# A decoder block on one core: input loads of the gates' stage ahead of weight stores, and the projection's result stores on ScalarE's queue

## The chip, the core and the metric

The kernel runs on one core of a Trainium2 chip. A core has a matrix engine (TensorE, PE in the profile, with its weight loads as PEld), a vector engine (VectorE, DVE), a scalar engine (ScalarE, ACT), GpSimd (POOL) and SyncE (SP), which here does nothing but issue DMAs. Each engine works through its own instructions in order and waits on semaphores for the others. An instruction that issues a DMA stands in its engine's order like any other; the transfer itself is done by 16 DMA engines that all queues share. The metric is the device time of one launch in microseconds. Before the change the median of three runs is 2417.23 us (2416.68 to 2417.39).

## The reference, cut to what matters

One layer of a decoder, sequence 2048, width 1024, float32:

```python
h = rmsnorm(x, attn_norm)
z = h @ w_in              # pool channels | q | k | v | gate_pool | gate_attn
a = pool_mixer(u_pool, w_pool, pool_scale)       # windows 2, 4, 8, 16
b = swa_sink_attention(q, k, v, sinks)           # window 128, 16 heads, 2 kv heads
x = x + (g_pool * a + g_attn * b) @ w_out        # g_* = sigmoid(gates + b_gate)
h = rmsnorm(x, ffn_norm)
up = causal_depthwise_conv(h @ w_up, conv_w, conv_b)   # 2 x 2816 channels, width 3
x = x + (silu(gate) * val) @ w_down
```

The two places that the change touches are the product that gives the gates (`z[..., o4:]`, two halves of 1024 columns) and the product with `w_out` with the residual added.

## The kernel before

The sequence is worked in two chunks (c = 0, 1) of T = 1024 tokens, channels on the 128 partitions and tokens along the free axis. Every float32 product is done as three products of reduced-precision halves: ACT copies the high half of an operand (a CAST row), DVE subtracts it from the whole to get the low half, and PE multiplies, for each block of the contraction in turn, high by high, high by low and low (of the weights) by high. A weight or an input that reaches PE thus passes a load, ACT and DVE first. Stages per chunk: keys and values, attention items with pieces of other projections between them, the gates, the output projection, the convolved up projection, the down projection.

**Order and buffers.** A scheduler places the instructions of each engine by priorities and costs, from the order in which the program is written; what it decided is fixed at build time. Tiles come from pools, and a new tile takes a buffer of its pool as soon as the tile there before it has had its last reader; its load waits for that reader. The pools that matter: "U" (19 buffers of 1 MB: input tiles, split weights and split inputs), "M" (5), and "R" (3, raw weights on their way in). All loads and stores but GpSimd's accumulating ones go through `load` (L239), that is, in the order of SP's queue: a store that waits for its result holds every load written behind it.

**The gates' stage** (`gates`, L1418; `Gates` and `Up` are the unit of work). A unit is one block of 128 gate channels, `units` has the blocks 5, 2, 3, 0, 1 in chunk 0. A unit's two products (pool gate and attention gate, over 1024 tokens) are done as one Strassen-like scheme of seven products, named `one` to `seven`, of weights A11, A12, A22, S1 to S4 and of inputs B11, B21, B22, T1 to T4. The input halves T1 to T4 are sums of the four input tiles of the chunk (`xg`, two 128-channel blocks each), which are loaded again from `xT`, scaled by the norm's gain on ACT (`scale_input`, L1415), added on DVE (`right_t1`, L1144; `right_t2`, L1153; `right_t3`, L1160; `right_t4`, L1170) and split into halves (`parted`, L1043 on ACT and L1044 on DVE). Tiles 0 and 1 are loaded during the last attention items (`mixer`, n = 4 and 5), tiles 2 and 3 in `gates`. PE's first products there that need tiles 2 and 3 are `three` (with T2), `five` (T3) and `seven` (T4).

In chunk 0 the weight blocks of the first two units are made in the last attention items (`units[f].w.step`, in `mixer`) and written to DRAM (`store`), to be fetched again in chunk 1 without being split again. The weights' pieces: A11 with A12 (one U tile, stored as `kept_A`), A22 (an M tile, also `kept_A`), S3 with S2 and S1 with S4 (U tiles, `kept_S`). `store` writes every piece that is made and not yet written.

**The output projection** (`out_proj`, L1055). For n = 0, 1 (halves of 512 tokens) and m = 0 to 7 (blocks of 128 channels): get the split weights of block m, 24 matmuls into a PSUM bank, add half of it to the residual on DVE (L1096), scale on ACT (L1098), square on ACT (L650, for the next norm), store the 256 KB result to `x2d` (L1105, a row of L239 on SP). The raw weights of w_out arrive in R tiles some blocks ahead and are split by L245 (ACT, twice 512 columns) and L246 (DVE). In chunk 0 it also makes the blocks of two up-projection weights (loads `U<-w_up`, steps at L358 and L359, stores `kept_A`, `kept_S`). In the trace's names, the raw weights of m = 4, 5 and 6 of n = 0 are the R tiles 5006, 5053 and 5103, and the results of m = 2, 3 and 4 are the M tiles 5041, 5090 and 5136.

Of the kernel before, what the change touches and what calls it, by code (L numbers as in the profile page):

```python
# [218 lines left out]
def block_kernel(ctx: ExitStack, tc: tile.TileContext, x, xT, pos, vec, qkn, w_poolT, w_pool, w_q, w_kv,  # L219
                 w_gp, w_ga, w_out, w_up, w_down, outT):  # L220
    nc = tc.nc
    V, G, A = nc.vector, nc.gpsimd, nc.scalar
# [15 lines left out]
    def load(dst, src):  # L238
        nc.sync.dma_start(dst, src)  # L239
# [813 lines left out]
    x2d = dp.tile([8, P, T], F32, "x2d")  # L1053

    def out_proj(c, ms, mixes):  # L1055

        xg = [up_.tile([P, 2, T], F32, "U") for _ in range(4)]
        norms = []

        def residual(j):  # L1060
            load(xg[j], xT[2 * j * P:(2 * j + 2) * P, c * T:(c + 1) * T]
                 .rearrange("(k p) t -> p k t", p=P))

        residual(0)
        heads = [Kept(f) for f in PRE]
        for n in range(2):
            acc = fp.tile([P, 512], F32, "F")
            c_ = slice(n * 512, (n + 1) * 512)
            for m in range(KT):
                if n == 0 and m % 2 == 0 and m < 6:  # L1070
                    residual(m // 2 + 1)
                w = stream.get("out", m)
                for f, at in PRE.items() if c == n == 0 else ():
                    if m == at:
                        raw = up_.tile([P, 2, 8, P], F32, "U")
                        load(raw[:, 0], w_up[f])
                        load(raw[:, 1], w_up[FT + f])
                        made = Blocks([raw[:, 0], raw[:, 1]])
                    elif at < m < at + 3:
                        made.step(2)  # L1080
                    elif m == at + 3:
                        made.store(f)
                if n == 0 and m == 3:
                    mixes[0] = mixed(0)
                if n == 0 and m > 3:
                    ms[7 - m].append(parted(mixes.pop(7 - m)[:, :, N1]))
                if n == 1 and m >= 6:
                    heads[m - 6].fetch("A11", "A12")
                if n == 1 and m == 7:
                    stream.ahead().step(1)  # L1090
                po = ps.tile([P, 512], F32, "f")
                mm3(po, [(w[:, 0, k, :], w[:, 1, k, :], ms[k // 2][n][:, 0, k % 2, :],
                          ms[k // 2][n][:, 1, k % 2, :])
                         for k in (6, 7, 4, 5, 2, 3, 0, 1)])
                x2 = mp.tile([P, 512], F32, "M")
                V.scalar_tensor_tensor(x2, po, 0.5, xg[m // 2][:, m % 2, c_], op0=ALU.mult,  # L1096
                                       op1=ALU.add)
                A.activation(xg[m // 2][:, m % 2, c_], x2, AF.Identity,  # L1098
                             scale=vc[:, V_FN + m:V_FN + m + 1])
                if m < 7 or n == 0:  # L1100
                    square_in(acc, x2, m == 0)
                else:
                    sq = mp.tile([P, 512], F32, "M")
                    A.square(sq, x2)
                load(x2d[m][:, c_], x2)  # L1105
                stream.part(stream.used + 2)
                if n == 1 and m == 1:
                    norms[0]()
                if n == 1 and m == 3:
                    pb, b = norms[1](), {}  # L1110
                if n == 1 and m >= 3 and m < 7:
                    right_first(xg, b, m - 3, pb)

            accs = [acc, sq] if n else [acc]

            def stats(n=n, accs=accs):
                rstd(accs, r2[:, 4 * n:4 * n + 4])

            def whole(n=n):
                return spread(r2[:, 4 * n:4 * n + 4], None)  # L1120

            norms += [stats, whole]
        return xg, b, norms[2:], heads
# [281 lines left out]
    def load_input(c, j):  # L1405

        t = up_.tile([P, 2, T], F32, "U")
        load(t, xT[2 * j * P:(2 * j + 2) * P, c * T:(c + 1) * T]
             .rearrange("(k p) t -> p k t", p=P))
        return t  # L1410
# [7 lines left out]
    def gates(c, units, b, xg, last_probabilities, last_values, last_filler):  # L1418


        def weights(f, n):
            if f < len(units):
                if units[f].w is None:
                    units[f].w = stream.get("gates", units[f].f)
                w = units[f].w
                w.step(n)
                if c == 0 and f < 2:
                    w.store(units[f].f)
                if n and w.at == 4:
                    stream.fetch(stream.used + (1 if f + 1 < len(units) else 2))  # L1430

        def parts(f, *names):
            if c > 0:
                units[f].w.fetch(*names)

        u0, u1, u2 = units[:3]
        if c > 0:
            u2.one("t")
        else:
            weights(1, 1)  # L1440
            last_filler()
        last_probabilities()
        last_values(-2)
        run_later(9)
        right_t1(xg, b, None, (1,))
        if c > 0:
            u2.two()
        last_values(-1)
        run_later(9)
        xg += [load_input(c, j) for j in (2, 3)]  # L1450
        parts(0, "S3", "S2")
        parts(1, "S3", "S2")
        if c > 0:
            weights(2, 1)
        u0.four()
        u0.early()
        for j in (2, 3):
            scale_input(xg[j], j)
        parts(0, "A22")
        t2s = right_t2(xg, b, None)  # L1460
        u1.four("a")
        u1.early()
        right_t3(xg, b)
        u0.three()
        u0.six()
        weights(2 if c > 0 else 1, 1)
        u0.five()
        right_t4(xg, b, t2s)
        parts(1, "A22")
        u0.fetch()  # L1470
        u1.three()
        u1.six()
        u0.attn()
        u0.seven()
        u0.value()
        if c == 0:
            weights(2, 1)
        u1.five()
        u0.combine()
        weights(2, 1)  # L1480
        n = len(units)
        for f in range(2, n):
            u, old = units[f], units[f - 1]
            if f > 2 or c == 0:
                u.one()
                u.two()
            if f == 2 and c == 0:
                weights(2, 2)
            old.fetch()
            old.attn()  # L1490
            weights(f + 1, 1)
            if f == n - 1:
                mixes = {j: mixed(j) for j in (3, 2, 1)}
            old.seven()
            old.value()
            weights(f + 1, 1)
            u.three()
            u.four()
            old.combine()
            if f == n - 1:  # L1500
                ms = {j: [parted(mixes[j][:, :, N0])] for j in (3, 2, 1)}
                x0 = up_.tile([P, 2, 2, 512], F32R, "U")
                old.parts(x0)
                stream.part(stream.used + 2)
            weights(f + 1, 1)
            u.five()
            u.early()
            u.six()
            weights(f + 1, 1)
        u.fetch()  # L1510
        u.attn()
        u.value(N1)
        u.seven()
        u.value(N0)
        for c_ in (N0, N1):
            u.combine(c_)
            if c_ == N0:
                u.parts(x0)
        ms[0] = [x0]
        return ms, mixes  # L1520
# [144 lines left out]
    def mixer(c, hs, kvw):  # L1665
# [48 lines left out]
        xg = []  # L1714
        for i in range(len(items)):
# [15 lines left out]
            if group == 3:  # L1731
                if c == 0:
                    if n == 0:
                        stream.fetch(stream.used + 2)
                    for f, steps in enumerate(({1: 1, 2: 2, 3: 1}, {5: 1, 7: 1})):
                        if n in steps:
                            with tc.issue_after(chain):
                                units[f].w.step(steps[n])
                            units[f].w.store(units[f].f)
                    if n == 4:  # L1740
                        stream.fetch(stream.used + 1)
                elif n < 5:
                    if n == 2:
                        stream.fetch(stream.used + 2)
                    if n > 2:
                        units[n - 3].w = Kept(units[n - 3].f)
                        units[n - 3].w.fetch("A11", "A12")
                elif n == 5:
                    units[2].w = stream.get("gates", units[2].f)
                    units[2].w.step(1)  # L1750
                else:
                    units[n - 6].w.fetch("S1", "S4")
# [118 lines left out]
```

## Time and profile before

| | us |
|---|---|
| median of 3 runs | 2417.23 |
| the profiled execution | 2413.23 |
| its span, first to last instruction | 2411.5 |
| PE busy | 2374.3 (98%) |
| DVE busy | 1886.6 (78%) |
| ACT busy | 1180.3 (49%) |
| POOL busy | 176.4 (7%) |
| mean DMA share over 380 to 440 / 505 to 600 | 0.64 / 0.80 |

Engine times are busy times within the span of one profiled execution. A row of the timeline gives the start and length in microseconds, the engine (SPq is the queue of SyncE), the line, the operation, the tiles out and in with their shapes, the count of like instructions that were put together, and in brackets the idle time before the row with what ended it. A row of the windows gives the window, its length, then busy time and count of PE, PEld, DVE, ACT and POOL, the granted clock of PE (1.00 is full speed), the DMA engines' share and GB/s. Times are from the span's start.

### The profile page before, as it was taken

What the parts mean: (1) busy time and instruction counts of PE and PEld (TensorE: products, weight loads), DVE (VectorE), ACT (ScalarE), POOL (GpSimd) and SP (SyncE); (2) the same over time, 40 slices, a digit from 0 to 9 for tenths busy, and PEclk for the clock granted to TensorE, in tenths of its full rate; (3) what the DMA queues carried; (4) which work ended last, traced back from release to release, by engine and by line L of the source; (5) the groups of instructions that cost most, each with busy time, mean ns of one, the idle gap of its engine ahead of it and who ended that gap; (6) DMA issues with size and microseconds to landing.
All of it is one profiled execution on the core that took longest, in us unless ns stands there. A gap on an engine that the chain in (4) does not pass through costs nothing.

```text
span 2411.5 us, 30292 instructions
## 1 busy us (share of the span) xinstructions
PE 2374.3 (98%) x11120; PEld 1969.9 (82%) x11120; DVE 1886.6 (78%) x2916; ACT 1180.3 (49%) x2169; POOL 176.4 (7%) x122
## 2 busy tenths in 40 slices
PE   8999998999999999999999999999999999999999
PEld 7888887777888888888888888888888888888887
DVE  8687886967877777799955877788588777779994
ACT  7455454555555555543522543455445445554431
POOL 1123121000000000000002142200000000000000
PEclk9999999999999999999999999999999999999999
DMA  9767777596322233546234576667642222228421
GB/s 342 244 199 239 228 216 259 173 348 246 104 99 79 88 107 116 178 163 205 88 140 156 165 223 183 197 208 242 208 158 93 93 80 79 79 71 288 140 70 53
DMA packets 160165, 400.77 MB, mean 166 GB/s; under 512 B 13840, under 2 KB 50192, under 8 KB 150288
## 3 DMA queue, kind: packets, MB, share of 16 engines
q1 hardware_dynamic: 155232, 390.25, 47.7%
q0 software_dynamic: 4352, 8.39, 2.2%
q8 instruction: 87, 1.43, 0.2%
q14 instruction: 62, 0.51, 0.1%
q10 hardware_dynamic: 432, 0.19, 0.0%
HBM read 264.17 MB, written 134.61 MB: 165 GB/s over the span
## 4 chain that ended last, share of the span: by engine, by line
PE 55%; DVE 1%; DMA 1%; ACT 0%; issue 0%; POOL 0%; SPq 0%; DVEq 0%; ACTq 0%; POOLq 0%
PE f L262 12%; PE f L1177 12%; PE t L1177 7%; PE f L1646 4%; PE a L1646 4%; PE s L1646 4%; PE t L1646 4%; PE a L1177 4%; PE a L934 1%; PE a L262 1%; PE s L873 1%; PE t L906 1%; DMA U<-made_pg 0%; DVE F L990 0%; ACT Q L892 0%; DMA U<-w_down 0%
## 5 line engine op out<-in xcount | busy, mean ns | idle before, releaser
L262 PE MATMUL f<-U,U 128*128 128x512 f32 (+1 forms) x2856 | 668.6, 390 | 11.1 <-ACT U L245 6.3
L262 PEld LDWEIGHTS f<-U,U 128*128 128x128 f32 x2856 | 524.6, 188 | 121.0 <-ACT U L245 7.5
L1177 PE MATMUL f<-U,U 128*128 128x512 f32 x1872 | 449.9, 391 | 9.6 <-ACT U L1043 7.5
L1177 PEld LDWEIGHTS f<-U,U 128*128 128x128 f32 x1872 | 352.6, 189 | 85.8 <-ACT U L1043 7.9
L1243 DVE SCALAR_TENSOR_TENSOR M<-F,vc,M 128x1024 f32<-128x1024 f32 x176 | 225.1, 1281 | 140.5 <-ACT M L1240 140.2
L1177 PE MATMUL t<-U,U 128*128 128x512 f32 x1332 | 315.0, 390 | 0.5 <-ACT Q L1195 0.4
L1177 PEld LDWEIGHTS t<-U,U 128*128 128x128 f32 x1332 | 249.5, 188 | 53.9 <-ACT Q L1195 1.2
L358 ACT CAST U<-R 128x1024 fp32r<-128x1024 f32 x147 | 153.5, 1053 | 81.9 <-DVE R L379 40.0
L1177 PE MATMUL a<-U,U 128*128 128x512 f32 x756 | 184.3, 390 | 1.4 <-ACT Q L1195 1.4
L359 DVE TENSOR_TENSOR U<-R,U 128x1024 fp32r<-128x1024 f32 x147 | 179.0, 1221 | 1.4 <-ACT U L358 1.4
L1177 PEld LDWEIGHTS a<-U,U 128*128 128x128 f32 x756 | 141.2, 188 | 31.6 <-ACT Q L1195 2.3
L1177 PE MATMUL f<-U,M 128*128 128x512 f32 x624 | 151.0, 389 | 0.3 <-DVE F L1221 0.3
L892 ACT ACTIVATE Q<-s,st,rq 128x128 f32<-128x128 f32 x256 | 114.0, 456 | 65.6 <-DVE st L889 61.1
L1177 PEld LDWEIGHTS f<-U,M 128*128 128x128 f32 x624 | 117.0, 188 | 25.0 <-DVE F L1221 0.8
L914 POOL TENSOR_SCALAR_AFFINE_SELECT M<-M 128x1024 fp32r<-128x1024 f32 x64 | 94.4, 1475 | 379.4 <-DVE st L894 213.3
L1229 ACT COPY F<-f 128x512 f32<-128x512 f32 x52 | 30.6, 588 | 184.1 <-PE f L1177 183.9
L1604 ACT CAST U<-U 128x1024 fp32r<-128x1024 f32 x76 | 79.0, 1051 | 83.4 <-PE s L1646 21.6
L1240 ACT ACTIVATE M<-F,vc 128x1024 f32<-128x1024 f32 x88 | 109.4, 1243 | 2.0 <-DVE F L1225 0.5
L1605 DVE TENSOR_TENSOR U<-U,U 128x1024 fp32r<-128x1024 f32 x76 | 91.9, 1218 | 3.5 <-ACT U L1604 3.2
L1604 ACT CAST F<-U 128x1024 fp32r<-128x1024 f32 x44 | 46.2, 1051 | 93.7 <-PE a L1646 64.0
L941 ACT COPY U<-a 128x512 f32<-128x512 f32 x64 | 37.5, 586 | 107.1 <-PE a L934 106.9
L246 DVE TENSOR_TENSOR U<-R,U 128x512 fp32r<-128x512 f32 x122 | 82.9, 705 | 9.0 <-ACT U L245 8.7
(283 smaller groups left out, 3715.2 us busy)
## 6 DMA issues: line engine op xcount, KB each, us to landing
R<-w_up SPq DMA_DIRECT2D x80, 512.0 KB, 3.7
actd<-M SPq DMA_DIRECT2D x44, 512.0 KB, 2.6
U<-w_down SPq DMA_DIRECT2D x88, 256.0 KB, 4.9
U<-actd SPq DMA_DIRECT2D x88, 256.0 KB, 5.2
qd<-U SPq DMA_DIRECT2D x64, 256.0 KB, 3.8
Q<-qd SPq DMA_DIRECT2D x64, 256.0 KB, 4.8
U<-xT SPq DMA_DIRECT2D x16, 1024.0 KB, 8.6
R<-w_out SPq DMA_DIRECT2D x32, 512.0 KB, 4.8
```

Source lines behind the costliest of these rows:

```text
L246: low = V.tensor_sub(lo[:, t], src[:, t], hi[:, t].bitcast(F32))
L262: nc.tensor.matmul(out, a, b, start=(i == 0), stop=(i == n - 1))
L358: A.copy(t[:, 0], raw)
L359: V.tensor_sub(t[:, 1], raw, t[:, 0].bitcast(F32))
L892: A.activation(pr[:, h, :], sc[:, h, 0:P], AF.Exp, bias=nm[:, h:h + 1], scale=it["rq"][:, h:h + 1], accum_out=rs[:, h:h + 1])
L914: G.affine_select(own.rearrange("p a h q -> p (a h) q"), pa.bitcast(F32).rearrange("p a h q -> p (a h) q"), pattern=[[0, 8], [1, P]], base ...
L1177: nc.tensor.matmul(bank, a[:, x, k, :], b[k // 2][:, y, k % 2, :], start=(first and i == 0), stop=(i == 11), skip_group_check=True)
L1240: A.activation(y, u[:, 2:], AF.Identity, bias=cw[:, 3, m:m + 1], scale=cw[:, 2, m:m + 1])
L1243: V.scalar_tensor_tensor(y, u[:, j:j + T], cw[:, j, m:m + 1], y, op0=ALU.mult, op1=ALU.add)
L1604: A.copy(hi, src)
L1605: V.tensor_sub(lo, src, hi.bitcast(F32))
L1646: nc.tensor.matmul(into[m], u[:, 0, c_], v[:, 1], start=(first and j == 0), stop=(k == n - 1 and j == 2), skip_group_check=True)
```

## The change

Three edits. First, the store of each of the projection's 32 results (16 per chunk) is issued by ACT instead of SP. Second, in chunk 0 the loads of input tiles 2 and 3 are written at the beginning of `gates`, ahead of the second unit's next weight step and of its stores, and no longer after the last attention values. Third, in the last attention items the second unit's blocks are no longer stored as they are made; the next `store` of this unit, in `weights(1, 1)` of `gates`, writes them together.

```diff
--- before.py
+++ after.py
@@ -1102,7 +1102,7 @@
                 else:
                     sq = mp.tile([P, 512], F32, "M")
                     A.square(sq, x2)
-                load(x2d[m][:, c_], x2)
+                A.dma_start(x2d[m][:, c_], x2)
                 stream.part(stream.used + 2)
                 if n == 1 and m == 1:
                     norms[0]()
@@ -1437,6 +1437,7 @@
         if c > 0:
             u2.one("t")
         else:
+            xg += [load_input(c, j) for j in (2, 3)]
             weights(1, 1)
             last_filler()
         last_probabilities()
@@ -1447,7 +1448,8 @@
             u2.two()
         last_values(-1)
         run_later(9)
-        xg += [load_input(c, j) for j in (2, 3)]
+        if c > 0:
+            xg += [load_input(c, j) for j in (2, 3)]
         parts(0, "S3", "S2")
         parts(1, "S3", "S2")
         if c > 0:
@@ -1736,7 +1738,8 @@
                         if n in steps:
                             with tc.issue_after(chain):
                                 units[f].w.step(steps[n])
-                            units[f].w.store(units[f].f)
+                            if f == 0:
+                                units[f].w.store(units[f].f)
                     if n == 4:
                         stream.fetch(stream.used + 1)
                 elif n < 5:
```

How this moves the instructions. SP's queue at the end of chunk 0's attention and the head of its gates, before:

```order
L239 DMA kept_A_40_4049<-U_4046 128x2048
L239 DMA U_4051<-xT 128x2x1024
L239 DMA dd_209<-F_4054 128x1024
L239 DMA R_4378<-w_ga 128x1024
L239 DMA kept_A_41_4205<-M_4200 128x1024
L239 DMA kept_S_42_4218<-U_4215 128x2048
L239 DMA xd_210<-U_3569 128x512
L239 DMA tad_208<-U_4087 64x4x512
L239 DMA U_4278<-xT 128x2x1024
L239 DMA U_4280<-xT 128x2x1024
```

and with the change, from the load of tile 1 on:

```order
L239 DMA U_4049<-xT 128x2x1024
L239 DMA dd_209<-F_4052 128x1024
L239 DMA kept_A_40_4218<-U_4046 128x2048
L239 DMA R_4378<-w_ga 128x1024
L239 DMA U_4209<-xT 128x2x1024
L239 DMA U_4211<-xT 128x2x1024
L239 DMA kept_A_41_4220<-M_4198 128x1024
L239 DMA kept_S_42_4222<-U_4215 128x2048
L239 DMA xd_210<-U_3569 128x512
L239 DMA tad_208<-U_4085 64x4x512
```

Input tiles 2 and 3 (`U_4278` and `U_4280` before, `U_4209` and `U_4211` now) stand behind the load of a gate weight (`R_4378`) now, and ahead of the second unit's stores (from `U_4046`, an M tile and `U_4215`), of the mixed result `xd` and of an attention store `tad`. Tile 1 (`U_4051`, now `U_4049`) stands ahead of the `U_4046` store. Since they ask for their buffers earlier, tiles 2 and 3 get others: tile 2 the one that the last score matmuls read (L873), tile 3 that of `U_3716`, which GpSimd's accumulating store (L946) reads.

DVE at the same place, where T2 to T4 are summed; a row with - is of before, one with + of the change, and the rest are in both:

```order
+L1153 TENSOR_TENSOR M_4313<-U_4209,U_3975 128x1024
+L1160 TENSOR_TENSOR U_3975<-U_4209,U_3975 128x2x512
+L1153 TENSOR_TENSOR M_4318<-U_4211,U_4049 128x1024
 L1044 TENSOR_TENSOR U_4315<-M_4313,U_4315 128x1024
-L1160 TENSOR_TENSOR U_4051<-U_4280,U_4051 128x2x512
+L1160 TENSOR_TENSOR U_4049<-U_4211,U_4049 128x2x512
 L1044 TENSOR_TENSOR U_4320<-M_4318,U_4320 128x1024
 L1044 TENSOR_TENSOR U_4351<-U_3975,U_4351 128x1024
-L1044 TENSOR_TENSOR U_4355<-U_4051,U_4355 128x1024
+L1044 TENSOR_TENSOR U_4355<-U_4049,U_4355 128x1024
+L1170 TENSOR_TENSOR U_4209<-U_4209,M_4313 128x2x512
 L359 TENSOR_TENSOR U_4373<-R_3973,U_4373 128x1024
```

Ten operations now stand from the first T2 sum to the low half of the second unit's S1 and S4 (`U_4373`). The first T4 sum (L1170) is one of them, right ahead of that low half; before, it stood ahead of the second T2 sum.

The second place is ACT in chunk 0's projection, from the split of m = 4's weights (`R_5006`) to the scaling and the square of m = 4's result (`M_5136`); before:

```order
L245 CAST U_5048<-R_5006 128x512
L1098 ACTIVATE U_4912<-M_5041,vc_127 128x512
L650 ACTIVATE M_5044<-M_5041 128x512
L245 CAST U_5048<-R_5006 128x512
L1098 ACTIVATE U_4912<-M_5090,vc_127 128x512
L650 ACTIVATE M_5093<-M_5090 128x512
L1098 ACTIVATE U_4913<-M_5136,vc_127 128x512
L245 CAST U_5097<-R_5053 128x512 x2
L650 ACTIVATE M_5139<-M_5136 128x512
```

and with the change:

```order
L245 CAST U_5048<-R_5006 128x512 x2
L1098 ACTIVATE U_4912<-M_5041,vc_127 128x512
L650 ACTIVATE M_5044<-M_5041 128x512
L1105 DMA x2d_211<-M_5041 128x512
L1098 ACTIVATE U_4912<-M_5090,vc_127 128x512
L650 ACTIVATE M_5093<-M_5090 128x512
L1105 DMA x2d_211<-M_5090 128x512
L245 CAST U_5097<-R_5053 128x512 x2
L1098 ACTIVATE U_4913<-M_5136,vc_127 128x512
L650 ACTIVATE M_5139<-M_5136 128x512
L1105 DMA x2d_211<-M_5136 128x512
```

Each result has its store (`x2d`) behind its square. The split of m = 5's weights (`U_5097<-R_5053`) stood behind the scaling of m = 4's result and now stands ahead of it; the second half of m = 4's split has moved ahead of the scaling of m = 2's result in the same way. SP's queue is the same there but for the rows of `x2d`, which are gone.

## The prediction

> **What bounds the kernel now.** I read the page first: is there an engine with no time to give?
>
> ```profile
> span 2411.5 us, 30292 instructions
> PE 2374.3 (98%) x11120; PEld 1969.9 (82%) x11120; DVE 1886.6 (78%) x2916; ACT 1180.3 (49%) x2169; POOL 176.4 (7%) x122
> ```
>
> TensorE (PE) is. Anything gained must come out of its 37 us of idle time or out of time at a low clock. The list of PE's waits says where the idle time lies:
>
> ```profile
> PE f L1177 <- ACT U L1043: 7.5, 1, 7.5
> PE f L262 <- ACT U L245: 6.3, 3, 2.6
> ```
>
> The first is one wait. The timeline puts it in the head of the gates' stage of chunk 0, which is where the change moves loads:
>
> ```profile
> 409.18 2.59 SPq L239 DMA_DIRECT2D U<-xT  x2
> ...
> 413.70 3.02 PE L1177 MATMUL a<-U,U 128*128 128x512 f32 x12 [0.68 <-ACT Q L1195]
> ...
> 417.62 2.19 ACT L1415 ACTIVATE U<-U,vc 128x1024 f32<-128x1024 f32 x2 [3.98 <-DMA U<-xT]
> 419.90 1.23 DVE L1153 TENSOR_TENSOR M<-U,U 128x1024 f32<-128x1024 f32 x1 [11.83 <-ACT U L1415]
> ...
> 424.23 0.80 PE L1177 MATMUL f<-U,U 128*128 128x512 f32 x1 [7.51 <-ACT U L1043]
> ...
> 425.74 11.02 PE L1177 MATMUL f<-U,U 128*128 128x512 f32 x35 [0.72 <-DVE U L1044]
> ...
> 436.60 1.75 PE L1177 MATMUL f<-U,M 128*128 128x512 f32 x7
> ...
> 439.77 5.15 PE L1177 MATMUL f<-U,U 128*128 128x512 f32 x22
> ```
>
> It reads as one chain. SyncE's queue (SP) issues input tiles 2 and 3 at 409.18, ScalarE (ACT) scales them when they land (417.62), VectorE (DVE) has been idle 11.83 us for them, and PE 7.51 us. PE is slow afterwards too: 36 matmuls take 12.37 us (424.23 to 436.60), where 22 take 5.15 us at 439.77, about 0.227 each. The windows of the trace name the cause, in the granted clock (the column before DMA share and GB/s):
>
> ```profile
> 424.00:426.00 2.00, 1.05 (x2) 0.55 (x3) 2.00 (x3) 1.59 (x3) 0.00 (x0) 0.50 0.09 36
> 430.00:432.00 2.00, 2.00 (x6) 1.22 (x6) 1.91 (x3) 0.59 (x1) 0.00 (x0) 0.70 0.00 0
> 432.00:434.00 2.00, 2.00 (x10) 1.62 (x10) 2.00 (x3) 0.00 (x0) 0.00 (x0) 1.00 1.03 389
> ```
>
> At full clock 36 x 0.227 = 8.2 us, so 4.2 us went there, the second wait of 0.72 included. With 7.51 and the 0.68 of row 413.70 the head loses **12.4 us**, the upper bound of the first term.
>
> The other place is the output projection of the same chunk:
>
> ```profile
> 504.83 24.87 PE L262 MATMUL f<-U,U 128*128 128x512 f32 x109
> 532.26 13.46 PE L262 MATMUL f<-U,U 128*128 128x512 f32 x48 [2.56 <-ACT U L245]
> 546.51 0.70 PE L262 MATMUL f<-U,U 128*128 128x512 f32 x2 [0.79 <-DVE M L1096]
> 547.62 5.29 PE L262 MATMUL f<-U,U 128*128 128x512 f32 x22 [0.40 <-DVE U L246]
> 554.82 0.73 PE L262 MATMUL f<-U,U 128*128 128x512 f32 x2 [1.90 <-ACT U L245]
> 555.90 10.71 PE L262 MATMUL f<-U,U 128*128 128x512 f32 x46 [0.35 <-DVE U L246]
> ```
>
> Between 529.70 (504.83 + 24.87) and 555.90 stand 74 matmuls; at 0.227 they need 16.8 us and took 26.2. So **9.4 us** are lost here: 6.0 in waits, 3.4 at a low clock. Three more windows: in chunk 1 the same stage has nothing to give (PE busy 109.34 of 110 us), and in chunk 0 the DMA engines are full (share 1.02 and 1.03) and the clock is down behind the first of these waits:
>
> ```profile
> 1690.00:1800.00 110.00, 109.34 (x497) 90.19 (x495) 70.94 (x91) 50.30 (x81) 2.05 (x2) 1.00 0.54 185
> 534.00:536.00 2.00, 2.00 (x6) 1.52 (x6) 0.93 (x1) 0.00 (x0) 0.00 (x0) 0.50 1.02 406
> 515.00:525.00 10.00, 10.00 (x45) 8.26 (x44) 7.57 (x11) 4.56 (x7) 0.00 (x0) 1.00 1.03 393
> ```
>
> **The change, part by part.** First term, the loads. They go from behind three stores that wait for DVE, and one that waits for ACT, to a place right behind a load of gate weights. When can they start, and does their landing beat the need?
>
> ```profile
> 380.13 1.62 SPq L239 DMA_DIRECT2D U<-xT  x1
> ...
> 383.67 1.02 POOL L946 DMA_DIRECT2D tad<-U  x1 [6.26 <-DMA tad<-U]
> ...
> 387.95 1.11 PE L873 MATMUL s<-U,Q 128*128 128x256 f32 x8
> ...
> 401.87 1.05 ACT L358 CAST U<-R 128x1024 fp32r<-128x1024 f32 x1 [4.28 <-DVE R L387]
> ...
> 404.35 1.06 ACT L1043 CAST U<-U 128x1024 fp32r<-128x1024 f32 x1
> ```
>
> ```profile
> U<-xT SPq DMA_DIRECT2D x2, 1024.0 KB, 8.8
> tad<-U POOLq DMA_DIRECT2D x1, 512.0 KB, 10.1
> ```
>
> Taken earlier from their pool, the tiles get other buffers, and so other waits. Tile 2 gets the buffer that the last score matmuls read: free at 389.06 (387.95 + 1.11), landed 8.8 us later at 397.9. ACT comes to its scaling about then and was idle 4.28 us before 401.87, so a wait there delays nothing. Tile 3's buffer is free when GpSimd's accumulating store has landed: 383.67 + 10.1 = 393.8, and with 8.8 more the tile is there at 402.6. ACT comes to it behind the cast of 404.35 and one more scaling, at about 406.5: 3.9 us of slack. DVE was idle from 408.07 (419.90 - 11.83), so it can begin the second group of sums there, 11.8 us sooner. Behind tile 3's wait on SP stands only a store that could not go before 398.8.
>
> What takes the stall's place? In the new order DVE does ten operations, started 1.14 us apart (row 419.90: 1.23 long, overlapping by 0.09), before the low half of block 1's second-product weights is done: 408.07 + 11.4 = 419.5. PE reaches the matmul that needs it at 416.0 (413.70 + 3.02 less the 0.68) + 12 x 0.227 + 2 x 0.227 = 419.2. A wait of 0.3, and of about 0.6 for ACT's copy behind it, is left. Tile 1 (380.13) also leaves before the store that it stood behind; its scaling and first sum then come ahead of the last probabilities on ACT and DVE, 1.15 + 1.14 us that hide behind PE's 24 matmuls of the last gate half (5.4 us at 0.227) and would cost that much without them. First term: 12.4 - 0.9 = **11.5 us**, between 12.4 and, with nothing hidden, 0.
>
> The stores of the second block do not become late: nothing in this chunk reads them back, and they leave once SP has issued tile 3, the same bytes in a stretch that has room:
>
> ```profile
> 380.00:400.00 20.00, 20.00 (x100) 16.36 (x99) 15.90 (x31) 12.69 (x30) 3.21 (x3) 1.00 0.69 222
> ```
>
> 222 GB/s over 20 us, against the 393 that row 515 shows, leaves 3.4 MB; the two tiles are 2 MB.
>
> Second term, the 32 result stores of the projection, from SP to ACT. What they held up on SP:
>
> ```profile
> 520.46 1.34 SPq L239 DMA_DIRECT2D kept_S<-U  x2
> ...
> 525.01 0.32 SPq L239 DMA_DIRECT2D x2d<-M  x1
> ...
> 526.87 1.35 SPq L239 DMA_DIRECT2D R<-w_out  x1
> ```
>
> ```profile
> 530.46 0.72 ACT L1098 ACTIVATE U<-M,vc 128x512 f32<-128x512 f32 x1 [4.19 <-DVE M L1096]
> 531.09 1.12 ACT L245 CAST U<-R 128x512 fp32r<-128x512 f32 x2
> ...
> 538.44 1.14 ACT L245 CAST U<-R 128x512 fp32r<-128x512 f32 x2 [4.77 <-DMA R<-w_out]
> ```
>
> The weights of m = 6 were issued at 526.87, behind the store of m = 3's result, and split at 538.44. The weights of m = 5 (531.09) were split late for another reason: ACT first waited for the result of m = 4. The new order has that split ahead of it, so the 2.56 us go, and with them the low clock (48 matmuls in 13.46 us instead of 10.9 + 0.2: 2.4 us): 5.0 us. The weights of m = 6 must then come about 5 us sooner; without the store of 525.01 they leave SP about 5 us earlier (right behind the stores of block 0's parts, 520.46 + 1.34 = 521.8), so they can; but these two stores, the pooled tile and the residual tile, 1 MB each, are still on their way in front of them, some 10 us at 393 GB/s, so I leave 1 us of new wait. The three short waits after 546 stay: their DVE work is the same.
>
> The price: 32 issues on ACT. The rows bound one from below (SP's for these stores) and give ACT's own:
>
> ```profile
> L239 SPq DMA_DIRECT2D x2d<-M x32: 319/323/327, 512.3 to 1773.1; - x32
> L428 ACTq DMA_DIRECT2D posi<-pos x1: 408/408/408, 0.8 to 0.8; - x1
> ```
>
> 0.41 us x 16 = 6.6 us per projection, in some 95 us of which ACT works about half. The upper bound is 1.62, the longest SP issue quoted. I take 0.41, hidden where ACT waits for results anyway (4.19 and 4.77 above). Queued behind a store on ACT are the next weight split, for which PE waits, and the next scaling. Second term: 5.0 - 1.0 = **4.0 us**, between 9.4 and below nothing (rival D).
>
> The sum, on the profiled execution: 2413.2 - 11.5 - 4.0 = 2397.7. That execution lies 4.0 us under the median of the three runs shown; from the median, 2417.2 - 15.5 = **2401.7 us**.
>
> [...]
>
> **Rivals.**
> A, the forecast: both terms, 2401.7.
> B, only the first: in the projection the DMA engines are the limit (share 1.03 at 515 to 525, 1.02 at 534 to 536), the same bytes pass, and PE's wait moves from m = 5 to m = 6. Time: 2417.2 - 11.5 = 2405.7. Against it: m = 6's weights were issued late, not only served late.
> [...]
> C, the change does only half of what it says: tile 3 comes late, since its buffer hangs on GpSimd's accumulate and the traffic has grown. From 406.5 on each us late is a us of PE. At 5 us late, with about 2.4 for the clock, the first term is 4.1: 2417.2 - 4.1 - 4.0 = 2409. Against it: 3.9 us of slack.
> D, slower: the stores on ACT's in-order queue. If an issue takes long while the engines are full, each store holds the weight split behind it. It decides from (11.5 + 4.8) / 32 = 0.51 us per store on PE's path. At half of 32 x 1.62 on the path: 2417.2 - 11.5 + 25.9 = 2431.6. Against it: SP's issues of these same stores were never above 0.327.
>
> **Chances.** A 0.52, B 0.30, C 0.13, D 0.05. A's own range runs from 2396 (both upper bounds would give 2395.4) to 2405; the range for all reaches past B and C: 2396 to 2411. No change means within 0.2% or 4.8 us here, about what measurement can tell. Below 2412.4 lie A, B and most of C: faster 0.92, same 0.04, slower 0.04.
>
> **What would show it.** First term right: the input loads stand near 389 and 394 in SP's queue, no PE wait over 1 us on L1043, clock 1.00 through 430, and the group of row 436.60 at about 425. Second: no wait of 2.56 at m = 5 and PE's row 555.90 about 15.5 us sooner, not 11.5. Wrong, if ACT waits in L1415 past 407, or if PE's waits on L245 grow.

## The result and the profile after

| | us |
|---|---|
| forecast | 2401.7 (2396 to 2411) |
| before, median of 4 runs | 2416.95 |
| changed, median of 4 runs (2399.76 to 2400.28) | 2399.97 |
| ratio | 0.9933, 95% interval 0.9916 to 0.9950 |
| profiled execution, before and changed | 2413.23 and 2400.09 |
| its span, before and changed | 2411.5 and 2398.4 |

The kernel became 0.5 to 0.8% faster. The total is close to the forecast; its split is not, as the two places show. The timeline of PE gives three marks that every version has: the last 24 matmuls of the attention's fillers, the start of the projection's first matmuls, and the first norm sum of the projection (L629). The 12 matmuls of the last gate product stand among the projection's, behind its first 5 (before) or 3 (changed). Before:

```profile
396.14 5.60 PE L262 MATMUL a<-U,U 128*128 128x512 f32 x24
...
499.62 1.30 PE L262 MATMUL f<-U,U 128*128 128x512 f32 x5
...
566.45 0.95 PE L629 MATMUL a<-one,F 128*128 128x1 f32 x8
```

And with the change:

```profile
395.84 5.61 PE L262 MATMUL a<-U,U 128*128 128x512 f32 x24
...
415.10 3.33 PE L1177 MATMUL f<-U,U 128*128 128x512 f32 x14
418.61 5.30 PE L1177 MATMUL f<-U,U 128*128 128x512 f32 x22 [0.17 <-DVE U L359]
423.74 2.88 PE L1177 MATMUL f<-U,M 128*128 128x512 f32 x12
...
486.30 0.84 PE L262 MATMUL f<-U,U 128*128 128x512 f32 x3
...
489.70 32.12 PE L262 MATMUL f<-U,U 128*128 128x512 f32 x141
526.29 14.03 PE L262 MATMUL f<-U,U 128*128 128x512 f32 x48 [4.46 <-ACT U L245]
540.68 0.73 PE L262 MATMUL f<-U,U 128*128 128x512 f32 x2 [0.36 <-ACT U L245]
542.36 10.74 PE L262 MATMUL f<-U,U 128*128 128x512 f32 x46 [0.94 <-DVE U L246]
552.94 0.95 PE L629 MATMUL a<-one,F 128*128 128x1 f32 x8
```

From the first mark to the second ("gates" below) it was 103.48 us and is 90.46: **13.0 us** gained. From the second to the third ("projection") it was 66.83 and is 66.64: **0.2 us** gained. The 0.30 by which this execution was ahead at the first mark, less 0.41 lost after the third, complete the 13.1 us between the spans.

In the gates' head the waits of 7.51 and 0.72 us are gone, one of 0.17 is left, and PE's clock stays up, where it was 0.50 and 0.70 in the same windows before:

```profile
424.00:426.00 2.00, 2.00 (x10) 1.66 (x9) 1.73 (x3) 1.58 (x2) 0.00 (x0) 1.00 0.34 131
430.00:432.00 2.00, 2.00 (x11) 1.65 (x10) 2.00 (x3) 0.00 (x0) 0.00 (x0) 1.00 0.03 8
```

In the projection the wait of 2.56 us at the weights of m = 5 is gone, since 3 + 141 = 144 matmuls, six groups of 24, now run through. In its place stands a wait of 4.46 us at m = 6, with 48 matmuls in 14.03 us behind it, 3.0 more than the 11.1 they take at 0.227 each and 0.16 for the end (from 22 in 5.15 us in the profile before); the clock was 0.50 from 526 to 532. SP's queue in this stretch, the landing of the weights of m = 6 (issued at 511.33), and their split on ACT, which waited for it:

```profile
504.50 1.45 SPq L239 DMA_DIRECT2D kept_S<-U  x2
506.86 0.37 SPq L239 DMA_DIRECT2D U<-xd  x1
510.12 0.38 SPq L239 DMA_DIRECT2D U<-xT  x1
511.33 0.37 SPq L239 DMA_DIRECT2D R<-w_out  x1
514.71 0.89 SPq L239 DMA_DIRECT2D U<-w_up  x2
```

```profile
R<-w_out SPq DMA_DIRECT2D x1, 512.0 KB, 13.7
```

```profile
525.10 1.14 ACT L245 CAST U<-R 128x512 fp32r<-128x512 f32 x2 [5.76 <-DMA R<-w_out]
```

The DMA engines are full for the 20 us around it:

```profile
505.00:515.00 10.00, 10.00 (x46) 8.29 (x45) 5.72 (x9) 3.78 (x7) 0.00 (x0) 1.00 1.02 421
515.00:525.00 10.00, 6.82 (x31) 5.31 (x29) 2.61 (x3) 2.19 (x3) 0.00 (x0) 1.00 1.03 412
```

So the load was issued 10.5 us before PE came to need it (at 521.8) and was still late: 13.7 us for 512 KB.

It was also issued later than the program's order alone would have it. Ahead of the residual's tile (510.12) SP stood 2.8 us for the landing of a result store that ACT had issued; the list of SP's waits between 507 and 510.3 us (us in total, times, longest) and ACT's row of that store show it:

```profile
SPq L239 <- DMA x2d<-M: 2.8, 1, 2.8
```

```profile
500.98 0.33 ACTq L1105 DMA_DIRECT2D x2d<-M  x1
```

The store of 500.98 took 9.1 us to land, that is until 510.1, and the residual's tile left at 510.12. The weights of m = 6 then waited 0.8 us more for a store of `kept_A`. So a store that ACT issued held SP here; what ties SP's issue to that store, the list does not tell.

### The profile page after: what moved, and what is told of

Its sections match the earlier page's. It is cut to its first block, busy times and chain, and to the rows that moved or that the text cites. A ratio compares the mean times of both kernels' runs of the same rounds, so it can differ in the third digit from the quotient of the medians.

```text
span 2398.4 us, 30265 instructions
## 1 busy us (share of the span) xinstructions
PE 2371.2 (99%) x11120; PEld 1970.5 (82%) x11120; DVE 1886.5 (79%) x2916; ACT 1179.5 (49%) x2169; POOL 176.2 (7%) x122
## 4 chain that ended last, share of the span: by engine, by line
PE 55%; DMA 1%; DVE 1%; ACT 1%; issue 0%; SPq 0%; POOL 0%; DVEq 0%; ACTq 0%; POOLq 0%
PE f L262 12%; PE f L1177 11%; PE t L1177 7%; PE f L1648 4%; PE a L1648 4%; PE s L1648 4%; PE t L1648 4%; PE a L1177 4%; PE a L934 1%; PE a L262 1%; PE s L873 1%; PE t L906 1%; DMA U<-made_pg 0%; DMA R<-w_out 0%; DVE F L990 0%; ACT Q L892 0%
```

## The experiments

Times are medians, with the ratio to the kernel before as it was timed beside the run. The marks of all profiled executions are in one table, gates and projection as defined above. In e3_early and e4_stores the whole last gate product stands ahead of the projection, and the second mark is the start of that product, so that in every row the projection holds the same 252 matmuls:

| run | median | ratio (interval) | gates | projection |
|---|---|---|---|---|
| before | 2416.95 | 1 | 103.48 | 66.83 |
| the change | 2399.97 | 0.9933 (0.9916 to 0.9950) | 90.46 | 66.64 |
| e1_loads | 2400.83 | 0.9942 (0.9929 to 0.9954) | 90.47 | 65.42 |
| e2_act | 2415.18 | 0.9999 (0.9990 to 1.0008) | 104.48 | 66.43 |
| e3_early | 2403.11 | 0.9949 (0.9936 to 0.9963) | 90.68 | 67.71 |
| e4_stores | 2410.70 | 0.9982 (0.9973 to 0.9991) | 99.06 | 67.09 |
| e5_order | 2399.24 | 0.9928 (0.9915 to 0.9940) | 90.46 | 66.09 |
| e6_block | 2398.90 | 0.9926 (0.9914 to 0.9938) | 90.46 | 63.60 |
| e7_half | 2398.04 | 0.9926 (0.9912 to 0.9939) | 90.46 | 62.20 |
| e8_store | 2392.57 | 0.9901 (0.9888 to 0.9915) | 90.47 | 57.63 |
| e8_again | 2391.49 | 0.9905 (0.9891 to 0.9918) | 90.46 | 57.13 |
| e10_sp | 2396.82 | 0.9925 (0.9913 to 0.9938) | 90.46 | 63.28 |
| e11_first | 2400.20 | 0.9940 (0.9927 to 0.9954) | 90.46 | 68.72 |
| e12_two | 2402.49 | 0.9948 (0.9935 to 0.9962) | 90.47 | 67.77 |

The gates' length repeats to 0.02 us in all ten profiles that have both moves of the head. Before was timed in four series, the first for the result, the others for e1_loads to e4_stores, for e5_order to e8_store and for the rest. Its medians lie between 2415.0 and 2417.0, and its single executions, but for one of 8813 us, between 2413.1 and 2418.2, so a difference of 2 us between medians of two series says little; the marks say more.

### The parts of the change

The change without the stores on ACT:

```diff
-                A.dma_start(x2d[m][:, c_], x2)
+                load(x2d[m][:, c_], x2)
```

> The change without its first edit: the loads of input tiles 2 and 3 early and the second unit's stores late, but the projection's 32 result stores on SyncE's queue as before. Theory 1 (the head of the gates gave everything, the stores on ScalarE nothing): about 2400 us, within 1 us of the whole change, a first seven-product at 424 +- 1 us in the trace and 9 to 10 us still lost in chunk 0's projection. Theory 2 (the prediction's split, 4 us of the gain come from the stores on ScalarE): about 2404 us.

Only the stores on ACT:

```diff
-                load(x2d[m][:, c_], x2)
+                A.dma_start(x2d[m][:, c_], x2)
```

> The kernel before with only the first edit: 32 result stores on ScalarE's queue. Theory 1 (no worth): within 1 us of the kernel before; PE's wait at the weights of m = 5 (2.56 us) goes and one of 4 to 5 us at those of m = 6 takes its place, with the clock at 0.5 behind it. Theory 2: 4 us faster than before. Theory 3 (the issues on ScalarE cost something and the loads pay for it): slower than before by more than 1 us.

Theory 1 held in both: e1_loads has the whole gain, e2_act has none. The head of e2_act is that of before, and PE's long wait there was 8.5 us where before's profile has 7.5: this stall differs by 1 us between executions, so the 13.0 us hold for one pair of profiles. In e2_act's timeline the wait stands where it stands in the changed kernel, at m = 6, and the load of these weights takes as long:

```profile
541.93 12.93 PE L262 MATMUL f<-U,U 128*128 128x512 f32 x48 [4.30 <-ACT U L245]
```

```profile
R<-w_out SPq DMA_DIRECT2D x1, 512.0 KB, 14.2
```

Then the two moves of the gates' head, one at a time. Only the loads early:

```diff
         else:
+            xg += [load_input(c, j) for j in (2, 3)]
             weights(1, 1)
             last_filler()
...
-        xg += [load_input(c, j) for j in (2, 3)]
+        if c > 0:
+            xg += [load_input(c, j) for j in (2, 3)]
```

> The kernel before with only the second edit: input tiles 2 and 3 loaded at the beginning of the gates, the second unit's stores where they were. In SyncE's queue tile 1 stays behind the store of A11 and A12, tiles 2 and 3 stand ahead of the stores of A22 and of S3 and S2. Theory 1 (only the two loads' place counts): 13 us faster than before, as e1_loads. Theory 2 (the moved stores are needed too, since tile 1 behind a store delays the sums and the store's bytes delay tile 2): 5 to 10 us faster, with a PE wait of 2 us or more at the first product with T2.

Only the second unit's stores late:

```diff
-                            units[f].w.store(units[f].f)
+                            if f == 0:
+                                units[f].w.store(units[f].f)
```

> The kernel before with only the third edit: the second unit's stores later, the two loads where they were written. In SyncE's queue tile 2 then stands ahead of the store of S3 and S2, tile 3 still behind it and behind the stores of xd and tad. Theory 1 (the later of the two loads decides): 0 to 3 us faster, tile 3 issued at 408 to 409 us as before, a PE wait of 4 to 7 us. Theory 2 (half of the tiles early is half of the gain): 6 us faster.

The loads' place alone shortens the gates by 12.8 of the 13.0 us, with no PE wait in the head above 0.35 us: theory 1 for the head. That the whole run is 2 us longer than e1_loads' is in its projection (67.71 against 65.42). The two differ by the third edit alone, which is in the gates; no run shows why the projection differs. The late stores alone give 4.4 us of 13.0. Tile 2 then comes early, but tile 3 is issued at 408.43 as before, and PE waits for its sums:

```profile
408.43 0.56 SPq L239 DMA_DIRECT2D U<-xT  x1
```

```profile
421.65 0.79 PE L1177 MATMUL f<-U,U 128*128 128x512 f32 x1 [4.22 <-ACT U L1043]
423.98 6.38 PE L1177 MATMUL f<-U,U 128*128 128x512 f32 x19 [1.53 <-DVE U L1044]
```

The wait is within theory 1's bounds, the gain a little above its 3 us.

### Why the stores on ACT gave nothing: place or bytes

Same bytes, another place: the weights of m = 6 ahead of the residual's last tile.

```diff
-                if n == 0 and m % 2 == 0 and m < 6:
-                    residual(m // 2 + 1)
+                if n == 0 and m in (0, 2, 5):
+                    residual((m + 1) // 2 + (m < 5))
```

> The whole change, and the residual's last tile asked for at m = 5, not at m = 4: in SyncE's queue the weights of m = 6 (and the up weights) then stand ahead of that 1 MB load, which waits for a buffer that PE reads. The same bytes. Theory Q (m = 6's weights are late by their place behind this load): PE's wait at m = 6, 4.5 us in the changed kernel, falls below 1.5 us, and the time by 4 to 8 us with the clock that goes with it. Theory D (the stretch is bound by bytes, and what stands ahead in the order only changes who waits): the wait stays above 3 us or comes back at the next weights or at the last result, time within 2 us of the whole change.

The weights of m = 6 now landed after 10.9 us and PE passed m = 6 without a wait. It stopped one group later instead, behind 3 + 165 = 168 matmuls, seven groups of 24, which is at m = 7:

```profile
532.66 0.73 PE L262 MATMUL f<-U,U 128*128 128x512 f32 x2 [4.16 <-ACT U L245]
533.96 19.08 PE L262 MATMUL f<-U,U 128*128 128x512 f32 x70 [0.57 <-DVE U L246]
```

The projection took 66.09 us against 66.64: theory D, the order only chose who waits. The expectation's reason for the residual's late issue, a buffer that PE reads, is not what the trace of the changed kernel shows: there SP waited for the landing of a result store, as told above.

The second block of up weights out of the first half:

```diff
-                for f, at in PRE.items() if c == n == 0 else ():
+                for f, at in () if c else ((n, 0),):
```

> The whole change, and the second block of up weights made in the projection's second half (n = 1, m = 0 to 3), not in the first: 1 MB of loads and 3.5 MB of stores leave the crowded stretch, the weights of m = 6 keep their place in the queue. Theory D (bytes): the weights of m = 6 share the engines with 1 MB less, so PE's wait there falls from 4.5 to about 2 us, the waits of 0.4 and 0.9 us behind go; 4 to 7 us faster than the whole change. Theory Q (place in the queue): the wait at m = 6 stays near 4.5 us, at most 2 us faster.

Mixed. The waits behind m = 6 went, as D had it, and the projection became 3.0 us shorter (1.1 us in the medians, where D had 4 to 7). The wait at m = 6 stayed, as Q had it:

```profile
526.73 23.58 PE L262 MATMUL f<-U,U 128*128 128x512 f32 x96 [4.64 <-ACT U L245]
550.14 0.95 PE L629 MATMUL a<-one,F 128*128 128x1 f32 x8
```

The weights of m = 6 took 13.1 us to land without the 1 MB of `w_up` that the changed kernel issues 3.4 us behind them, and 13.7 us with it. So what came after this load had hardly slowed it, and D had to be narrowed to what is issued ahead of it.

Fewer bytes ahead, the same place:

```diff
-                        made.store(f)
+                        made.store(f, 1)
...
-                    done[names] = dp.tile(list(t.shape), F32, f"kept_{f}_{names[0]}")
-                    load(done[names], t.bitcast(F32))
+                    done[names] = dp.tile([P, part] + list(t.shape)[2:], F32, f"kept_{f}_{names[0]}")
+                    load(done[names], t.bitcast(F32)[:, 0:part])
```

> The whole change, and of each kept piece of the two up-weight blocks only the high half is stored (3.5 MB fewer in the projection, of which 1.75 MB ahead of the weights of m = 6); later it is fetched twice in place of the low half, so the low halves of these two weight blocks are left out of the up projection. No place in the queue of the projection changes. Theory D: 1.75 MB at about 0.4 MB per us is 4.4 us, so PE's wait at m = 6 all but goes, and the low clock with it: 5 to 9 us faster. Theory Q: the wait stays above 3 us and the time within 2 us of the whole change.

The wait at m = 6 is gone with no change of place, and the projection is 4.4 us shorter. The weights left SP 22.6 us behind the second mark (25.0 in the changed kernel), since SP stood still for 2.5 us behind the kept stores (505.38 to 507.90), where the changed kernel's SP waited 4.4 us for landings in all, and took 11.2 us to land, not 13.7. What is left is one wait of more than 1 us, at the start of n = 1, and the clock stayed up behind it:

```profile
536.25 0.73 PE L262 MATMUL f<-U,U 128*128 128x512 f32 x2 [1.92 <-ACT U L245]
537.93 10.73 PE L262 MATMUL f<-U,U 128*128 128x512 f32 x46 [0.95 <-DVE U L246]
```

```profile
538.00:540.00 2.00, 2.00 (x9) 1.66 (x10) 2.00 (x3) 2.00 (x5) 0.00 (x0) 1.00 0.65 167
```

That is D's mechanism. The size fell short of the 5 to 9 us, and the median moved by only 1.9 us, within what medians of two series differ by.

Both spread out: the second block in the second half, and each block's stores one step of m later, so that the weights of m = 6 stand ahead of all of them.

```diff
-                for f, at in PRE.items() if c == n == 0 else ():
+                for f, at in () if c else ((n, 0),):
...
-                    elif m == at + 3:
+                    elif m == at + 4:
                         made.store(f)
```

> As with the second block in the second half, and the stores of the first block asked for one step of m later, which puts the weights of m = 6 ahead of all four of these stores and of the last residual tile in SyncE's queue. Both theories agree that the weights of m = 6 come in time: no PE wait there over 1 us. Theory D: with the crowd spread over the stage no other takes its place, 7 to 10 us faster than the whole change (all of the 9.3 us that its projection loses). Theory Q, or a buffer that is held longer: a new wait of 2 us or more at the pooled tile or the residual, 3 us faster or less.

> The run e8_store once more, so that the next one has it beside it on the same chip: 2392 to 2394 us, and 57 +- 0.3 us from the last seven-product of the gates to the first norm sum of the projection.

No wait is left in the projection; the 237 matmuls behind the first three run in one row, and the weights of m = 6 land in 5.6 us. e8_again came out a little under what was expected of it: 2391.49 us, and 56.45 us from the last gate product (487.96), where e8_store had 56.95. From e8_again:

```profile
490.68 53.89 PE L262 MATMUL f<-U,U 128*128 128x512 f32 x237
544.41 0.95 PE L629 MATMUL a<-one,F 128*128 128x1 f32 x8
```

```profile
R<-w_out SPq DMA_DIRECT2D x1, 512.0 KB, 5.6
```

This is about all of the 9.4 us that the prediction had counted as lost in this stage. The kernel leaves nothing out, and it is 7 to 9 us faster than the change. Its DMA engines are as full over the 20 us in question as those of the changed kernel:

```profile
505.00:515.00 10.00, 10.00 (x46) 8.28 (x45) 8.17 (x12) 6.67 (x13) 0.00 (x0) 1.00 1.03 417
515.00:525.00 10.00, 10.00 (x46) 8.29 (x45) 4.32 (x7) 3.41 (x5) 0.00 (x0) 1.00 1.02 418
```

So full engines alone do not make PE wait. What counted here is how much is issued ahead of the load that PE needs next.

Only the first block's stores later:

```diff
-                    elif m == at + 3:
+                    elif m == at + 3 + (f == 0):
                         made.store(f)
```

> The whole change, and only the first block's four stores asked for one step of m later; the second block stays in the first half. Theory D (what is issued ahead of the weights of m = 6 makes them late): no wait over 1 us at m = 6; the second block's 1 MB load and 3.5 MB of stores still crowd the rest, so waits of 1 to 3 us come at m = 7 or at n = 1; projection 59 to 62 us where the changed kernel has 66, and 4 to 7 us faster. If the second block is what counts: projection 64 us or more, under 2 us faster.

A miss: m = 6 came in time, and the projection got longer, 68.72 us. The late transfer was now the raw up weights of the second block. ACT stands in order before their split, DVE stands before its half of the split, and the addition of the next result (L1096) stands behind that on DVE. From the timeline of PE, of ACT and of DVE:

```profile
533.07 7.32 PE L262 MATMUL f<-U,U 128*128 128x512 f32 x24 [4.92 <-DVE M L1096]
```

```profile
527.08 1.05 ACT L358 CAST U<-U 128x1024 fp32r<-128x1024 f32 x1 [5.81 <-DMA U<-w_up]
```

```profile
528.16 1.23 DVE L359 TENSOR_TENSOR U<-U,U 128x1024 fp32r<-128x1024 f32 x1 [5.47 <-ACT U L358]
```

The two halves of e8_store, each nearly alone (e6_block and e11_first), give 3.0 us and -2.1 us in the projection, and 9.0 to 9.5 us together.

### Is the first edit worth anything

The spread-out version with its result stores back on SP:

```diff
-                A.dma_start(x2d[m][:, c_], x2)
+                load(x2d[m][:, c_], x2)
```

> As e8_store, with the 32 result stores back on SyncE's queue. Theory 1 (the place of these stores is worth nothing by itself, the order of the 3.5 MB stores and loads is): within 1.5 us of e8_store and no PE wait over 1 us in chunk 0's projection. Theory 2 (with the crowd spread, the in-order wait on SyncE would show): the projection loses 2 to 5 us, PE waits for a weight split.

Here theory 2 held, a little above its price: 5.3 us slower than e8_again, timed beside it, and a projection of 63.28 us against 57.13. Stores of results stand ahead of the weights of m = 7 in SP's queue, and each holds what is behind it until its result is made, the last at 517.99. So these weights leave at 518.45, 4.2 us later against the second mark than in e8_again (514.40). ACT's order adds to it: it splits them at 530.02, behind the scaling and the square of a result, 0.9 us after they have landed (518.45 + 10.7), where in e8_again DVE's half of the split starts at 526.94, behind a wait of 1.40 us for ACT's. PE then waits at m = 7, and is slow behind it (72 matmuls in 19.39 us, 2.9 more than at 0.227 each and 0.16 for the end; the clock was 0.50 from 532 to 536):

```profile
517.99 0.37 SPq L239 DMA_DIRECT2D x2d<-M  x1
518.45 1.20 SPq L239 DMA_DIRECT2D R<-w_out  x1
```

```profile
531.19 19.39 PE L262 MATMUL f<-U,U 128*128 128x512 f32 x72 [3.09 <-ACT U L245]
```

So the mechanism of the prediction's second term exists, with about its size (5.0 us before the deduction). In the kernel as it is, the megabytes ahead of the weights of m = 6 hide it.

Twice as many issues on ACT:

```diff
-                A.dma_start(x2d[m][:, c_], x2)
+                for i in (0, 256):
+                    A.dma_start(x2d[m][:, n * 512 + i:n * 512 + i + 256], x2[:, i:i + 256])
```

> The whole change with each of the 32 results stored as two halves, 64 issues on ScalarE and the same bytes. If an issue on ScalarE costs its 0.33 us on PE's path (the trace's row), or if rival D of the prediction were near: 32 x 0.33 = 10 us slower than the whole change. If it is hidden in ScalarE's idle time: within 2 us of it.

The gates are unchanged, the projection is 1.1 us longer, the rest is not; the ratio's interval overlaps that of the change. So 32 more issues cost nothing near 10 us. They did push the weights of m = 6 back, to 32.5 us behind the second mark (25.0 in the changed kernel):

```profile
520.32 0.34 SPq L239 DMA_DIRECT2D R<-w_out  x1
```

SP stood still for 7.3 us ahead of this load, from the end of its row of 512.66 (0.38 long) to 520.32. Whether the landing of a store of ACT's ended this, as it ended the 2.8 us in the changed kernel, was not shown, and what the projection would gain without it is open, since no run took it away.

## Why the prediction was right, and where it was not

**The first term** had its mechanism right and its size 1.5 us small: 11.5 forecast, 13.0 measured. Tile 3 was not late (rival C). The queue let its load go at 395.9, not 394, but it landed in 5.2 us, at 401.1, and ACT scaled it when it came to it, without a wait. The loads' issues, the second one's landing, ACT's last scaling and DVE's first sum show it:

```profile
L239 SPq DMA_DIRECT2D U<-xT x2: 378/381/384, 388.8 to 395.9; - x2
```

```profile
U<-xT SPq DMA_DIRECT2D x1, 1024.0 KB, 5.2
```

```profile
406.95 1.18 ACT L1415 ACTIVATE U<-U,vc 128x1024 f32<-128x1024 f32 x1
```

```profile
407.13 1.21 DVE L1153 TENSOR_TENSOR M<-U,U 128x1024 f32<-128x1024 f32 x1
...
417.34 1.21 DVE L359 TENSOR_TENSOR U<-R,U 128x1024 fp32r<-128x1024 f32 x1
```

DVE began at 407.13 (forecast 408.07) and had the low half of the weights at 418.55 (forecast 419.5). PE came to need it at 418.44 (forecast 419.2), and the wait of 0.6 us set aside for ACT's copy did not show, so the wait was 0.17 and not 0.9. The other 0.8 us lie outside the sum, which counted from row 413.70 to the first seven-product and, with 0.17 of its 12.4 left, would give 12.2. Up to that product 12.56 us were gained (436.60 - 396.14 against 423.74 - 395.84), and 0.46 more behind it, which was not looked for there.

**The second term** failed: 4.0 forecast, 0.2 measured. Its first steps came true: the split of m = 5 ahead of ACT's wait took the 2.56 us away and the low clock (0.50 at 534 to 536 before) with it. The step that failed is "the weights of m = 6 leave SP about 5 us earlier, so they can; I leave 1 us of new wait". Two things were wrong in it. Against the second mark they left only 2.2 us sooner (27.25 us behind it before, 25.03 after), because the load ahead of them, the residual's last tile, went at 510.12 and not right behind the kept stores: SP waited 2.8 us for the landing of one of the very stores that had been moved to ACT, and 0.8 us for a kept store. These 3.6 us are more than what is missing of the 5. And they took 13.7 us to land, where those of before took 11.5:

```profile
R<-w_out SPq DMA_DIRECT2D x1, 512.0 KB, 11.5
```

They took 2.2 us longer, which is all of it back. The prediction had read both facts it needed, the share of 1.02 and 1.03 and the 1 MB transfers in front, and turned them into 1 us. This is **rival B** (chance 0.30), shown by e2_act, e5_order and e7_half, with its price: the wait moves from m = 5 to m = 6 and grows to 4.46 us with 3.0 at a low clock (0.50). The prediction's own sign of being wrong, growing waits on L245, showed too: 4.5 us before and 4.8 now between 440 and 600 us. B's reason, that the DMA engines are the limit, holds in a narrower form, since e8_again has the same share and no wait: it is the bytes issued ahead of these weights. The forecast's argument against it, that these weights were issued late, is right once those bytes are out of the way (e10_sp). How the 13.7 us and the 3.6 us of waiting on SP would share the loss, no run separates.

What the choice of queue was worth differed: in the change 0.2 us of the projection and in e2_act a ratio of 0.9999, but 5.3 us in e8_again against e10_sp, by the in-order wait that stands ahead of the next load and the order on ACT that comes with it.

**Why the sum came near** all the same: 1.5 us more in the first term, 3.8 less in the second, and a median of before that stood 3.7 us above the profiled execution, against which the two terms were made. The profiled executions differ by 13.1 us, the medians by 17.0. That part of the agreement is luck: before's executions spread over 5 us, and the first mark alone lies between 395.84 and 397.64 in the profiles of kernels that do nearly the same up to it. B's own sum, 2405.7, lies further from the 2399.97 measured than the forecast, though B is what the traces show in the projection.

**Rival D** (issues on ACT): 32 issues of 0.326 us, and no time on PE's path that could be seen, also when doubled.

```profile
L1105 ACTq DMA_DIRECT2D x2d<-M x32: 326/326/362, 498.6 to 1760.2; - x32
```

## What to carry to other kernels

Before a wait that is removed is counted as gained, look at the next entry of the same queue and at what is issued ahead of it: here, with a DMA share of 1.02 and 1.03 for 20 us and the freed load behind megabytes, a better place in the queue only changed who waits (4.46 us at m = 6, or 4.16 at m = 7 in e5_order). Put the bytes that nobody waits for behind that load first, and try the place again afterwards; e10_sp and e8_again show 5 us that could not be seen in the crowded version. When a store moves to another engine, look in the list of the queue's waits whether the old queue still waits for its landing, as SP did here for 2.8 us. And test the parts of a change one by one even if the total agrees with the forecast, since here one part was worth 13 us and the other nothing.

## What the runs showed of the hardware that was not expected

The length of one wait alone does not tell whether the clock falls. In e1_loads PE waited 1.53 us and, 5.3 us of work later, 1.92 us, and ran at 0.55 behind the second:

```profile
520.12 5.32 PE L262 MATMUL f<-U,U 128*128 128x512 f32 x22 [1.53 <-DVE U L246]
527.36 13.15 PE L262 MATMUL f<-U,U 128*128 128x512 f32 x48 [1.92 <-ACT U L245]
```

```profile
528.00:530.00 2.00, 1.92 (x5) 1.49 (x5) 1.51 (x3) 2.00 (x3) 0.00 (x0) 0.55 1.04 422
```

A wait of 1.92 us in e7_half, with 0.38 some 7 us ahead of it and 0.95 right behind two matmuls after it, left the clock at full speed (1.00 in the window 538 to 540, and 46 matmuls in 10.73 us, where 0.227 each and 0.16 for the end make 10.6). So the clock fell behind 1.53 and 1.92 with work between them (3.45 us in all, 0.55 in e1_loads) and behind 2.56 alone (0.50 in the kernel before), and did not behind 1.92 and 0.95 (2.87 in all, 1.00 in e7_half). What such a wait costs beside itself was 2.1 us in e1_loads and 2.9 in e10_sp and the changed kernel's 3.0, so a wait near 2 us can cost twice its length, and in e7_half it did not. What rule decides between these cases stays open.
